# Meta keys inside the diagonal key blocks, and half-stored weights, in a planner-ordered trunk kernel

## The chip, the cores and the metric

The kernel runs on one core of one Trainium2 chip. TensorE multiplies matrices from SBUF into PSUM, VectorE, ScalarE and GpSimd do the elementwise work, and SyncE and GpSimd issue the DMAs. In the profile these are PE (with PEld for its weight loads), DVE, ACT, POOL and SP. The metric is the device time of one execution in microseconds (us); lower is better.

## The reference

One layer (DEPTH = 1) over 2048 tokens of width 1024, with 16 learned meta tokens put ahead of them. A combined projection gives seven groups of 512 columns. Half of the channels pass through GLU, a causal depthwise convolution, LayerNorm, swish, a second projection and a gate; the other half through stick-breaking attention with 8 heads of 64. Both halves are then projected, normalised and added to the input.

```python
def hybrid_layer(h, ...):
    u = rms_norm(h, pre_g)
    glu_a, glu_b, conv_gate, q, k, v, sb_gate = split(u @ w_in)
    c = glu_a * sigmoid(glu_b)
    c = causal_depthwise_conv(c, conv_w, conv_b)          # width 31
    c = silu(layer_norm(c, conv_ln_g, conv_ln_b))
    c = (c @ w_pw2 + b_pw2) * silu(conv_gate)
    s = stick_breaking_attention(q, k, v) * silu(sb_gate)
    return h + rms_norm(concat([c, s]) @ w_out, post_g)

# stick breaking, for every head, strictly causal (s < t):
#   z[t,s] = q[t].k[s] / 8
#   A[t,s] = sigmoid(z[t,s]) * prod_{s<j<t} (1 - sigmoid(z[t,j])) ;  out[t] = sum_s A[t,s] v[s]
```

The 16 meta tokens are the oldest keys of every query. The output drops their rows.

## The kernel before

**Tiles.** The 2048 tokens are four chunks `c` of 512 (`TC`), each of four token blocks `r` of 128. Every f32 operand of a matrix product is held as a rounded high part and the rest, the low part (fp32r), and a product takes three matmuls (high*high, low*high, high*low); `mm3` does this for the projections with a stationary weight of 128x128 and 512 moving columns. A weight slab of 128x512 is four such stationary operands.

**Attention.** `weigh` (L1291) takes one head, one key chunk `kc` and one query block `r`: two matmuls (q high, q low against `kk`, the stacked high and low keys) into a PSUM tile `T`, a sigmoid on ACT in place, and a scan on DVE from the newest key to the oldest that forms the running product `pr`. In the diagonal chunk (`kc == c`) only the first 128(r+1) keys count. `flip` turns the products by four PE transposes into another `T` tile, ACT copies the high part `ah` out, DVE subtracts for the low part `al`, and `gather` multiplies both by the differences of the values (`vk`) into `av`. PSUM has eight banks: two `mm`, four `T`, one `av`, one `cv`.

**Meta keys.** They are handled apart. `meta_k` (L1060) loads the meta keys once into `km`. When a pair of heads' queries has been projected, `meta_scores` (L935) multiplies them with `km`: two matmuls of 512 columns into a `T` tile, an ACT copy and a DVE addition into `zt`. In unit `i == 2` of each chunk's attention `zt` is turned by four transposes and copied by DVE to `sgm` (L1465). After all heads of a chunk have been weighed, `meta_keys` (L1500), which runs during the next chunk, takes the sigmoid of `sgm` on ACT, continues the scan over the 16 keys (four scans on DVE), turns the result into one `T` tile `pt`, and for each of four pairs `j` of heads reads 32 rows of `pt` twice: ACT copies the high part into a tile `mixs`, DVE subtracts for the low part; POOL copies the high part once more. Then one matmul against `vm` (the meta values) per pair. In the last chunk this is done in parts of heads (`ehl` instead of `mixs`), and for the last two heads in `meta_late`, which uses `vl`.

**Weights.** A raw slab comes by DMA into one of `RAWS` = 4 buffers `wr`; ACT rounds it to the high part, POOL (at the very start DVE) subtracts for the low part. Slabs used in several chunks are written back to DRAM (`wscr`, 512 KB: both parts) when first split in chunk 1's projections or chunk 0's tail, and later loaded from there straight into a `w` buffer, four of which exist. `prepare` (L560) does this for the next slab whenever one is released.

**Order.** The order of instructions is made while the program is built. Work on the PE comes as streams of pieces; `merge` (L1867) picks between attention (`main`), the projections (`fill`) and the meta keys (`extra`) by when, by a simple clock model with one cost per operation, the data and PSUM tiles of the next piece will be there. What follows on the other engines is put off by `when(...)` and let go in the order of that clock. Engines run their own queue in order, so the model's mistakes show as waits. Any change of a cost, a buffer or an operation moves many instructions after it. The stages of the program overlap: while chunk `c` is in attention, the fill is the gate of `c`, the output projection of `c-1`, the convolution's tail of `c` and the input projection of `c+1`. In chunk 3 the fill ends with `out_part`, the output projection as far as its inputs are there; `last_room` gives it the buffers of the projection's input.

All engine calls pass through one helper, so nearly every row of the profile has line 218; rows are told apart by tile names (`mm<-uh,w` is a projection, `T<-kk,q` the scores, `T<-ident,pr` the turning, `av<-ah,vk` the gathering).

Of the kernel before, what the change touches and what calls it, by code (L numbers as in the profile page):

```python
# [19 lines left out]
P = 128  # L20
# [19 lines left out]
EV, WB, RAWS, PR, EHL = 5, 4, 4, 9, 4  # L40
# [46 lines left out]
class Clock:  # L87
# [3 lines left out]
    def __init__(self):  # L91
        self.ready, self.used, self.free, self.rings, self.bufs = {}, {}, {}, {}, {}
        self.dma = 0.0
        self.shared = {}
        self.soon = []

        self.here = ()
# [71 lines left out]
class Engine:  # L169
# [7 lines left out]
    def __getattr__(self, name):  # L177
        call = getattr(self.engine, name)

        def issue(out, *args, **kw):  # L180
# [11 lines left out]
            when = max([c.at(a) for a in near] + [c.free.get(out.name, 0.0)]) + self.wait  # L192
            if self.gap:
# [12 lines left out]
            done = self.now + late  # L206
            if name == "dma_start":
# [15 lines left out]
def pe_cost(name, n, kw):  # L223
    return (0.108 if name == "transpose" else max(n * 4.537e-4, 0.11)), 0.19
# [42 lines left out]
def trunk(ctx: ExitStack, tc: tile.TileContext, x, xturn, xlater, meta, cpack, post_g, wpack, out):  # L267
# [84 lines left out]
    both = const.tile([P, ncp + TC], F32, name="cp")  # L352
    cp, zt = both[:, : ncp + KD * NM], both[:, ncp:]
# [31 lines left out]
    vl = const.tile([P, 2, P], F32R, name="vl")  # L385
    km = const.tile([P, NJ, 3, 2 * NM], F32R, name="km")
    cm = const.tile([P, NTB, NH, MS], F32, name="cm")
    sgm = const.tile([P, NTB, NH, MS], F32, name="sgm")
    ct = [const.tile([P, HIST + TC], F32, name=f"ct{j}") for j in range(NJ)]

    def clear():
        for j in range(NJ):
            nc.gpsimd.memset(ct[j][:, 0 : HIST - NM], 0.0)
        nc.gpsimd.memset(km.bitcast(F32), 0.0)
        nc.gpsimd.memset(vm.bitcast(F32), 0.0)
        nc.gpsimd.memset(vl.bitcast(F32), 0.0)
        nc.gpsimd.memset(cm, 0.0)
        nc.gpsimd.memset(sgm, 0.0)
# [134 lines left out]
    wscr = dr.tile([len(again), P, 2, 4 * P], F32, name="wscr")  # L533
    place = {key: wscr[i] for i, key in enumerate(again)}
# [13 lines left out]
    whole = [key for key, n, kept, save in order if not kept]  # L548
# [11 lines left out]
    def prepare(most=WB):  # L560

        while most and todo_w:
# [14 lines left out]
            if kept and tag == "w":  # L577
                sp.dma_start(both.bitcast(F32), place[key][:, :, :n])
            elif kept:
                for i, t in ((0, hi), (1, lo)):  # L580
                    sp.dma_start(t.bitcast(F32), place[key][:, i, :n])
            else:
# [4 lines left out]
                def keep_it(key=key, both=both, lo=lo):  # L587
                    when(lambda: pool.dma_start(place[key], both.bitcast(F32)), [lo])

                split(raws.popleft(), hi, lo, dve if first else pool, keep_it if save else None)  # L590
# [305 lines left out]
    def qk_proj(c, g, scr, with_meta):  # L896
        for j in range(NJ):
# [37 lines left out]
    def meta_scores(j, hi, lo):  # L935

        pt = PT("T", [P, TC])
        for i, t in ((0, hi), (1, lo)):
            pe.matmul(
                pt[: 4 * NM], km[:, j, i : i + 2].rearrange("p i s -> p (i s)"), t[:, NM:],  # L940
                start=(i == 0), stop=(i == 1),
            )
        zj = zt[2 * j * NM : 2 * (j + 1) * NM]
        act.activation(zj, pt[: 2 * NM], AF.Copy)
        dve.tensor_tensor(zj, pt[2 * NM : 4 * NM], zj, op=ALU.add)
# [54 lines left out]
    def values(c):  # L1000
# [3 lines left out]
        for j in range(NJ):  # L1004
# [52 lines left out]
            if c == 0 and j == 0:  # L1057
                in_us(4.5, meta_k, outs=[km])

    def meta_k():  # L1060
        force("k")
        for e in range(2):
            rows = slice(e * HD, (e + 1) * HD)
            for i in range(2):
                sp.dma_start(
                    km[rows, :, 1 - i, e * NM : (e + 1) * NM].bitcast(F32),
                    kscr[e::2, i, :, 0:NM].rearrange("j d s -> d j s"),
                )

    def meta_v(h):  # L1070
# [8 lines left out]
        if h >= EARLY:  # L1079
            sp.dma_start(  # L1080
                vl[h * NM : (h + 1) * NM, :, e * HD : (e + 1) * HD].bitcast(F32),
# [175 lines left out]
    def load_k(h, kc):  # L1257
        force("k")
        s0 = NM + kc * TC
        kk = T("kk", [P, TC], 2, F32R)  # L1260
        sp.dma_start(
            kk.bitcast(F32), kscr[h, :, :, s0 : s0 + TC].rearrange("l d s -> (l d) s")
        )
        return kk

    def load_first(c, force=False):

        if ("first", c) not in keep and (force or (("q", c) in keep and ("z", c - 1) in keep)):
            keep["first", c] = load_q(c, 0), load_k(0, c)
# [5 lines left out]
    def attention(c, mixs):  # L1275
        heads = {}

# [13 lines left out]
        def weigh(u, r):  # L1291
# [7 lines left out]
            z = PT("T", [P, TC])  # L1299
            for i in range(2):  # L1300
                pe.matmul(
                    z[:, :wd], hd["q2"][:, i, r * P : (r + 1) * P], kk[:, :wd],
                    start=(i == 0), stop=(i == 1),
                )
            act.activation(z[:, :wd], z[:, :wd], AF.Sigmoid, scale=-SCALE)
            pr = T("pr", [P, TC], PR)
            dve.tensor_tensor_scan(
                pr[:, :wd][:, ::-1], z[:, :wd][:, ::-1],
# [122 lines left out]
        for i in range(len(order) + 1):  # L1431
            u = None
            if i < len(order):
                h, kc = order[i]
                u = dict(h=h, kc=kc, diag=kc == c, kk=kk, a=[], at=[])
                if i + 1 < len(order):
                    if c == 0:
                        heads[h + 1] = load_q(c, h + 1)
                    kk = load_k(*order[i + 1])
                    if 0 < kc == c and h + 1 < NH:  # L1440
                        heads[h + 1] = load_q(c, h + 1)
            for b in range(NTB if u else len(flips)):
                if u:
                    yield need(heads[u["h"]]["q2"], u["kk"], tag="T")
# [593 lines left out]
```

## Time and profile before

| | |
|---|---|
| three runs | 1309.15, 1309.17, 1310.23 us; median 1309.17 |
| profiled execution | 1310.28 us, of it 1308.5 us span of the core |
| mean granted TensorE clock | 0.997 |
| DMA traffic | 300.83 MB, 230 GB/s on average |
| HBM written | 77.46 MB |

In the page, "busy" of an engine is the share of the span in which an instruction of it ran; matmuls are pipelined, so the PE's rows overlap and a matmul's own duration (some 0.39 us for 512 columns) is longer than the distance between two starts. That distance is read from the timeline. A row of the timeline gives the start, the length, the engine, line and operation, the tile written and the tiles read, the shape and the count of merged instructions; in brackets stands the idle time of the engine just before, and what ended it. A row of the groups gives the count, the busy time, the mean of one in ns, and after a second bar the idle time before these instructions with the releasers.

### The profile page before, as it was taken

Reading aid. Unit: us, or ns where it says so; the run is one execution under the profiler, and the core shown is the slowest. Engines: PE = TensorE matmul, PEld = TensorE weight load, DVE = VectorE, ACT = ScalarE, POOL = GpSimd, SP = SyncE. Lnnn points to the kernel's source line nnn. Section 1 sums busy time; section 2 is a strip of 40 time slices with the busy share of each in tenths; the row PEclk is TensorE's granted clock in tenths of the full one; section 3 lists DMA queues with packets and bytes.
Section 4 is the critical chain, followed back from the end, with each engine's and each line's share of the span. In section 5 each row is a group of like instructions: output and inputs, shape, how many; then the busy total and the mean of one; then the engine's idle time right before and its main releaser. Section 6 shows DMA issues by size and latency. Waiting matters only on the chain.

```text
span 1308.5 us, 21884 instructions
## 1 busy us (share of the span) xinstructions
PE 1284.4 (98%) x7442; PEld 1106.4 (85%) x7442; DVE 1019.2 (78%) x1446; ACT 743.0 (57%) x1477; POOL 690.4 (53%) x820
## 2 busy tenths in 40 slices
PE   8999999999899999999999999999999999999897
PEld 8998888888799878888789988888887899888797
DVE  5999999999873588974676578985558988898964
ACT  6544455444555452676645544688785666755543
POOL 3555568767687430878762232599887221321402
PEclk9999999999999999999999999999999999999999
DMA  6687877899868986667756696667666456586555
GB/s 234 216 277 236 264 252 258 300 348 314 287 218 285 322 289 199 202 214 231 252 166 194 193 344 208 184 197 215 213 200 213 138 157 199 180 259 212 177 164 183
DMA packets 166400, 300.83 MB, mean 230 GB/s; under 512 B 17280, under 2 KB 71744, under 8 KB 166288
## 3 DMA queue, kind: packets, MB, share of 16 engines
q1 hardware_dynamic: 152496, 251.44, 61.8%
q0 software_dynamic: 13792, 47.98, 9.5%
q8 instruction: 59, 0.97, 0.3%
q14 instruction: 53, 0.43, 0.1%
HBM read 221.90 MB, written 77.46 MB: 229 GB/s over the span
## 4 chain that ended last, share of the span: by engine, by line
PE 87%; DVE 5%; ACT 2%; DMA 2%; issue 2%; POOL 1%; SPq 1%; DVEq 0%; POOLq 0%; ACTq 0%
PE mm L218 57%; PE T L218 20%; PE av L218 9%; DVE pr L218 2%; DVE ul L218 1%; ACT ev L218 1%; DMA w<-wscr 1%; DVE sgm L218 1%; DMA wr<-wpack 1%; DVE tok L218 1%; SPq L218 1%; DVE mixs L218 0%; DMA qscr<-ehl 0%; POOL w L218 0%; PE cv L218 0%
## 5 line engine op out<-in xcount | busy, mean ns | idle before, releaser
L218 PE MATMUL mm<-uh,w 128*128 128x512 f32 (+1 forms) x1936 | 563.7, 377 | 1.1 <-ACT uh L218 1.1
L218 PEld LDWEIGHTS mm<-uh,w 128*128 128x128 f32 x1936 | 336.7, 188 | 53.5 <-ACT uh L218 1.7
L218 PE MATMUL mm<-ul,w 128*128 128x512 f32 (+1 forms) x968 | 357.6, 371 | 0.1
L218 DVE TENSOR_TENSOR al<-T,ah 128x512 fp32r<-128x512 f32 (+1 forms) x320 | 191.7, 599 | 119.2 <-ACT ah L218 117.8
L218 DVE TENSOR_TENSOR_SCAN pr<-T,pr,zcol 128x512 f32<-128x512 f32 x192 | 245.2, 1277 | 44.4 <-ACT T L218 42.8
L218 ACT ACTIVATE ah<-T 128x512 fp32r<-128x512 f32 (+1 forms) x320 | 170.1, 532 | 178.0 <-PE T L218 176.2
L218 DVE SCALAR_TENSOR_TENSOR cv<-ct,cp,cv 128x512 f32<-128x512 f32 x319 | 239.1, 749 | 7.0
L218 ACT ACTIVATE T<-T 128x512 f32<-128x512 f32 (+2 forms) x320 | 167.7, 525 | 84.3 <-PE T L218 73.9
L218 POOL TENSOR_TENSOR acc<-acc,pd 128x512 f32<-128x512 f32 x150 | 194.9, 1299 | 34.3 <-ACT pd L218 26.6
L218 POOL TENSOR_TENSOR w<-wr,w 128x512 fp32r<-128x512 f32 x132 | 171.2, 1303 | 75.2 <-ACT w L218 72.8
L218 PEld LDWEIGHTS mm<-ul,w 128*128 128x128 f32 x968 | 181.6, 188 | 33.6 <-DVE ul L218 0.5
L218 PE MATMUL T<-kk,q 128*128 128x512 f32 (+3 forms) x640 | 194.2, 386 | 3.7 <-DVE pr L218 2.6
L218 PE MATMUL T<-ident,pr 128*128 128x128 f32 x1088 | 171.9, 273 | 2.1 <-DVE al L218 1.1
L218 PEld LDWEIGHTS T<-ident,pr 128*128 128x128 f32 x1088 | 134.7, 141 | 33.7 <-DVE al L218 1.5
L218 PEld LDWEIGHTS T<-kk,q 128*128 128x128 f32 x640 | 105.9, 190 | 18.8 <-DVE pr L218 4.1
L218 DVE TENSOR_TENSOR_SCAN pr<-T,tri 128x128 f32<-128x128 f32 (+3 forms) x128 | 103.6, 814 | 22.9 <-ACT T L218 22.5
L218 ACT ACTIVATE pd<-ct,cp 128x512 f32<-128x512 f32 x150 | 106.7, 718 | 21.7 <-POOL acc L218 21.2
L218 PE MATMUL av<-ah,vk 128*128 128x512 f32 (+1 forms) x320 | 117.8, 368 | 0.0
L218 PE MATMUL av<-al,vk 128*128 128x512 f32 (+1 forms) x320 | 117.4, 367 | 0.0
L218 ACT ACTIVATE w<-wr 128x512 fp32r<-128x512 f32 x140 | 86.5, 626 | 33.7 <-POOL w L218 10.0
L218 POOL COPY cm<-pr 128x1 f32<-128x1 f32 x120 | 24.0, 200 | 131.7 <-DVE pr L218 131.1
L218 POOL TENSOR_TENSOR ev<-ev 64x512 f32<-64x512 f32 (+2 forms) x46 | 55.5, 1206 | 68.8 <-ACT ev L218 38.5
(210 smaller groups left out, 1609.7 us busy)
## 6 DMA issues: line engine op xcount, KB each, us to landing
w<-wscr SPq DMA_DIRECT2D x150, 512.0 KB, 4.1
wr<-wpack SPq DMA_DIRECT2D x140, 256.0 KB, 4.4
wscr<-w POOLq DMA_DIRECT2D x68, 512.0 KB, 5.0
kk<-kscr SPq DMA_DIRECT2D x80, 256.0 KB, 4.6
vk<-vscr SPq DMA_DIRECT2D x80, 256.0 KB, 3.9
q<-qscr SPq DMA_DIRECT2D x64, 256.0 KB, 5.8
vscr<-mixs SPq DMA_DIRECT2D x32, 256.0 KB, 3.4
qscr<-ehl SPq DMA_DIRECT2D x32, 256.0 KB, 3.4
```

The source lines that it names most:

```text
L218: return call(out, *args, **kw)
```

## The change

Five edits, which belong together in the building program:

1. **Meta keys as columns.** `km`, `zt`, `meta_k`, `meta_scores` and the turning of `zt` are gone. In the diagonal chunk `kk` gets 16 columns ahead of its 512, loaded from the same `kscr` (one DMA of 528 columns in chunk 0, where they are neighbours; a separate 16-column DMA in chunks 1 to 3). For `r` = 0, 1, 2 the score matmuls take 16 columns more in the same PSUM tile. For `r` = 3, where 512 columns fill the bank, each of the two parts has an extra matmul of 16 columns into a `T` tile of its own. ACT takes the sigmoid of the 16 columns straight into `sgm` (128x16), ahead of the large one; there are two `sgm`, one for even and one for odd chunks, and the later sigmoids over `sgm` are gone.
2. **Kept weights.** Of the input projection's kept slabs (all but the convolution gate's) only the low part is written (`lscr`, 256 KB) and read back; the raw slab is loaded again and ACT rounds it for the high part. The others keep both parts.
3. **Meta weights copied once.** For chunks 0 to 2 `meta_keys` copies `pt` to an SBUF tile (`turned`) by one ACT instruction of 128x512; high and low parts are formed from that.
4. **Five raw buffers** (`RAWS` = 5).
5. **Around them:** `vl` goes into unused rows of `vm`; in the last chunk the first part of `meta_keys` may begin when `last_room` has made room and waits for the convolution only before its matmuls, using two of that room's buffers; `out_part` takes the convolution's half of the first products for both token halves before the attention's half; the clock model lets an engine wait for another that holds the same PSUM bank, and prices a matmul by its own columns.

```diff
-EV, WB, RAWS, PR, EHL = 5, 4, 4, 9, 4
+EV, WB, RAWS, PR, EHL = 5, 4, 5, 9, 4
...
+            for b in banks:
+                who, end = c.last.get(b, (self, 0.0))
+                if who is not self:
+                    when = max(when, end)
...
+            if name == "matmul":
+                n = int(np.prod(out.shape[1:]))
...
-    return (0.108 if name == "transpose" else max(n * 4.537e-4, 0.11)), 0.19
+    return (0.108 if name == "transpose" else max(n * 4.537e-4, 0.11 if n > NM else 0.03)), 0.19
...
+    def low_alone(key):
+        return key[0] == w_in and key[1] // P // NJ * NJ != G_CG
...
-    whole = [key for key, n, kept, save in order if not kept]
+    whole = [key for key, n, kept, save in order if not kept or low_alone(key)]
...
+                raw = raws.popleft()
+                if kept:
+                    sp.dma_start(lo.bitcast(F32), place[key][:, :n])
+                    when(lambda raw=raw, hi=hi: act.activation(hi, raw, AF.Copy), [raw], [hi])
+                else:
+                    split(raw, hi, lo, dve if first else pool, keep_it if save else None)
...
-            if g == G_Q:
-                when(
-                    lambda a=(j, hi, lo): meta_scores(*a), [hi, lo], [zt], tag="T",
-                    date=pe.now + 4.0,
-                )
...
-            z = PT("T", [P, TC])
+            zb = PT("T", [P, TC])
+            o = NM if diag and wd < TC else 0
+            z, zr = zb[:, o : o + wd], zb[:, 0:NM]
+            if diag and not o:
+                zr = PT("T", [P, TC])[:, 0:NM]
             for i in range(2):
+                q = hd["q2"][:, i, r * P : (r + 1) * P]
+                if diag and not o:
+                    pe.matmul(zr, q, kk[:, 0:NM], start=(i == 0), stop=(i == 1))
                 pe.matmul(
-                    z[:, :wd], hd["q2"][:, i, r * P : (r + 1) * P], kk[:, :wd],
-                    start=(i == 0), stop=(i == 1),
+                    zb[:, : o + wd], q, kk[:, NM - o : NM + wd], start=(i == 0), stop=(i == 1)
                 )
-            act.activation(z[:, :wd], z[:, :wd], AF.Sigmoid, scale=-SCALE)
+            if diag:
+                act.activation(sgm[:, r, h, 0:NM], zr, AF.Sigmoid, scale=-SCALE)
+            act.activation(z, z, AF.Sigmoid, scale=-SCALE)
...
             if i == 2:
-                force(zt)
-                yield need(zt, tag="T")
-                pt = PT("T", [P, NTB, NH, NM])
-                for r in range(NTB):
-                    pe.transpose(
-                        pt[:, r].rearrange("p h s -> p (h s)"), zt[:, r * P : (r + 1) * P], ident
-                    )
-                dve.tensor_copy(sgm[:, :, :, 0:NM], pt)
...
+        turned = pt if part else T("ehl", [P, TC], EHL)
+        if not part:
+            act.activation(turned, pt, AF.Copy)
         for j in js:
-            src = pt[2 * j * NM : 2 * (j + 1) * NM]
+            src = turned[2 * j * NM : 2 * (j + 1) * NM]
...
-                for i in range(2):
-                    banks[i] = yield from out_products(
-                        w, mix, range(KD - 2), i, False, there=there
-                    )
+                for part in range(NJ), range(NJ, KD - 2):
+                    for i in range(2):
+                        banks[i] = yield from out_products(
+                            w, mix, part, i, False, banks[i], there
+                        )
```

Three places of the new order. First the PE where chunk 3's attention begins (one head's diagonal block, `q_...` being the queries), before:

```order
L218 MATMUL T<-kk,q_11175 128x256 x2
L218 MATMUL T<-kk,q_11175 128x384 x2
L218 MATMUL T<-kk,q_11175 128x512 x2
L218 MATMUL mm<-uh,w 128x512 x2
L218 MATMUL mm<-ul,w 128x512
L218 MATMUL mm<-uh,w 128x512 x2
L218 MATMUL mm<-ul,w 128x512
L218 MATMUL T<-ehl,km 64x512 x2
L218 MATMUL T<-kk,q_11175 128x512 x2
```

and the same place of the changed kernel:

```order
L228 MATMUL T<-kk,q_11477 128x272 x2
L228 MATMUL T<-kk,q_11477 128x400 x2
L228 MATMUL mm<-uh,w 128x512 x2
L228 MATMUL mm<-ul,w 128x512
L228 MATMUL mm<-uh,w 128x512 x2
L228 MATMUL mm<-ul,w 128x512
L228 MATMUL T<-kk,q_11477 128x16
L228 MATMUL T<-kk,q_11477 128x512
L228 MATMUL T<-kk,q_11477 128x16
L228 MATMUL T<-kk,q_11477 128x512 x5
```

The two matmuls against `km` have gone, the first three score pairs are 16 columns wider, and each half of the fourth has a 16-column matmul ahead of it.

Second, ACT where the meta weights of chunk 2 are taken out of PSUM (`mixs<-T 32x512` reads 32 rows of the turned tile; `ah` and `T<-T` are attention's own copies and sigmoids), before:

```order
L218 ACTIVATE ev<-mm 128x512
L218 ACTIVATE w<-wr 128x512
L218 ACTIVATE T<-T 128x512
L218 ACTIVATE mixs<-T 32x512 x4
L218 ACTIVATE ah<-T 128x512
L218 ACTIVATE T<-T 128x512
L218 ACTIVATE ah<-T 128x384
```

and now:

```order
L228 ACTIVATE w<-wr 128x512
L228 ACTIVATE pd<-ct_94,cp 128x512
L228 ACTIVATE ehl<-T 128x512
L228 ACTIVATE mixs<-ehl 32x512 x4
L228 ACTIVATE ah<-T 128x512
L228 ACTIVATE T<-T 128x512
L228 ACTIVATE ah<-T 128x384
```

One copy of the whole tile stands ahead, and the four pieces read SBUF instead of PSUM.

Third, the PE near the end, where head 7's diagonal block begins while the output projection fills in (`mm<-w,mixc` is the convolution's half of it, `mm<-wr,mixs` the attention's), before:

```order
L218 MATMUL mm<-w,mixc 128x256 x12
L218 MATMUL T<-ident,pr 128x128 x4
L218 MATMUL T<-kk,q_14065 128x128 x2
L218 MATMUL av<-ah,vk 128x512
L218 MATMUL av<-al,vk 128x512
L218 MATMUL T<-ident,pr 128x128 x4
L218 MATMUL T<-kk,q_14065 128x256 x2
L218 MATMUL av<-ah,vk 128x512
L218 MATMUL av<-al,vk 128x512
L218 MATMUL T<-ident,pr 128x128 x4
L218 MATMUL T<-ident,uh 128x128 x4
L218 MATMUL T<-kk,q_14065 128x384 x2
```

and now:

```order
L228 MATMUL mm<-w,mixc 128x256 x12
L228 MATMUL T<-ident,pr 128x128 x4
L228 MATMUL T<-kk,q_14432 128x144 x2
L228 MATMUL av<-ah,vk 128x512
L228 MATMUL av<-al,vk 128x512
L228 MATMUL T<-ident,pr 128x128 x4
L228 MATMUL mm<-w,mixc 128x256 x12
L228 MATMUL T<-ehl,vm 128x512
L228 MATMUL T<-ident,uh 128x128 x4
L228 MATMUL T<-kk,q_14432 128x272 x2
L228 MATMUL av<-ah,vk 128x512
L228 MATMUL av<-al,vk 128x512
```

Another group of twelve matmuls of the convolution's half now stands between the score blocks of this head.

More of the change, by code (lines that the diff above doesn't have):

```diff
@@ L94, in __init__ @@
         self.shared = {}
+        self.last = {}
         self.soon = []
@@ L192, in issue @@
             when = max([c.at(a) for a in near] + [c.free.get(out.name, 0.0)]) + self.wait
+            banks = [a.name for a in (*outs, *near) if a.space == PSUM]
+            for b in banks:
+                who, end = c.last.get(b, (self, 0.0))
+                if who is not self:
+                    when = max(when, end)
             if self.gap:
@@ L206, in issue @@
             done = self.now + late
+            for b in banks:
+                c.last[b] = self, self.now + 0.03
             if name == "dma_start":
@@ L351, in trunk @@
     ncp = NJ * CW + KD + 4 * NJ
-    both = const.tile([P, ncp + TC], F32, name="cp")
-    cp, zt = both[:, : ncp + KD * NM], both[:, ncp:]
+    cp = const.tile([P, ncp + KD * NM], F32, name="cp")
     cw = cp[:, 0 : NJ * CW].rearrange("p (j w) -> p j w", w=CW)
@@ L384, in trunk @@
     vm = const.tile([P, NJ, P], F32R, name="vm")
-    vl = const.tile([P, 2, P], F32R, name="vl")
-    km = const.tile([P, NJ, 3, 2 * NM], F32R, name="km")
     cm = const.tile([P, NTB, NH, MS], F32, name="cm")
-    sgm = const.tile([P, NTB, NH, MS], F32, name="sgm")
+    sgms = [const.tile([P, NTB, NH, MS], F32, name=f"sgm{i}") for i in range(2)]
     ct = [const.tile([P, HIST + TC], F32, name=f"ct{j}") for j in range(NJ)]
@@ L576, in prepare @@
                 hi, lo = (T(tag, [P, 4 * P], RAWS, F32R)[:, :n] for _ in range(2))
[L577 to L581, printed above, removed]
+            if kept and not low_alone(key):
+                if tag == "w":
+                    sp.dma_start(both.bitcast(F32), place[key][:, :, :n])
+                else:
+                    for i, t in ((0, hi), (1, lo)):
+                        sp.dma_start(t.bitcast(F32), place[key][:, i, :n])
             else:
@@ L1276, in attention @@
         heads = {}
+        sgm = sgms[c % 2]
         def load_v(h, kc):
@@ L1443, in attention @@
                 if u:
-                    yield need(heads[u["h"]]["q2"], u["kk"], tag="T")
+                    yield need(
+                        heads[u["h"]]["q2"], u["kk"], tag="T",
+                        n=2 if u["diag"] and b == NTB - 1 else 1,
+                    )
                     weigh(u, b)
@@ L1513, in meta_keys @@
             pool.memset(bm, 0.0)
+        sgm = sgms[c % 2]
         zm = sgm[:, :, hs, 0:NM]
-        act.activation(zm, zm, AF.Sigmoid, scale=-SCALE)
         for r in range(NTB):
@@ L1538, in fetch @@
         def fetch(j):
-            given[j] = [ev()[:, :TC] for _ in range(2)]
-            hold.update(t.name for t in given[j])
+            if j:
+                given[j] = [ev()[:, :TC] for _ in range(2)]
+                hold.update(t.name for t in given[j])
+            else:
+                given[j] = keep["first given"]
             bring(j)
@@ L1566, in meta_keys @@
             pool.tensor_copy(m[4 * NM : 6 * NM], m[high].bitcast(F32))
+        if part:
+            yield need(given=lambda: ("conv", c) in keep)
         for j in js:
@@ L1923, in last_room @@
         keep["bm"] = a[:, 4:6].rearrange("p e (b h s) -> p e b h s", b=NTB, h=NH)
+        keep["first given"] = a[:, 6], a[:, 7]
+        keep["room", c] = True
         pool.memset(a[:, 4:6], 0.0)
-        zm = sgm[:, :, EARLY:, 0:NM]
-        act.activation(zm, zm, AF.Sigmoid, scale=-SCALE)
         keep["pg"] = a[:, 2:4]
```

69 lines of the change are left out of this document (28 added, 41 removed).

## The prediction

> **What bounds the kernel now.** I read the page first: busy shares, slices, and the chain of work that ended last.
>
> ```profile
> PE 1284.4 (98%) x7442; PEld 1106.4 (85%) x7442; DVE 1019.2 (78%) x1446; ACT 743.0 (57%) x1477; POOL 690.4 (53%) x820
> ...
> PE   8999999999899999999999999999999999999897
> ...
> PE 87%; DVE 5%; ACT 2%; DMA 2%; issue 2%; POOL 1%; SPq 1%; DVEq 0%; POOLq 0%; ACTq 0%
> ```
>
> The PE is busy 98% of the span in every stage and holds 87% of the chain. So a microsecond is won in two ways only: by matmuls that go, or by moments in which the PE waits. What the other engines save counts where the PE waits for them. The waits of the PE, longest first in total, are short:
>
> ```profile
> PE T L218 <- DVE pr L218: 5.3, 6, 2.0
> PE T L218 <- DVE mixs L218: 4.2, 3, 2.5
> ```
>
> They are single events of up to 2.5 us, all for a tile `T`, so I looked each up in the timeline. The other terms are small too; a change here is worth about 1%.
>
> **Meta keys as columns: the PE's work.** The distance between starts, not a row's length, is what a matmul costs.
>
> ```profile
> 978.15 0.62 PE L218 MATMUL T<-ehl,km 128*64 128x512 f32 x2
> 978.61 0.62 PE L218 MATMUL T<-kk,q 128*128 128x512 f32 x2
> ...
> 1150.64 0.60 PE L218 MATMUL T<-ident,pr 128*128 128x128 f32 x4
> 1150.99 0.42 PE L218 MATMUL T<-kk,q 128*128 128x128 f32 x2
> 1151.25 0.44 PE L218 MATMUL av<-ah,vk 128*128 128x512 f32 x1
> ...
> L218 PE MATMUL T<-ehl,km 128*64 128x512 f32 x32 | 10.2, 399 | 2.5 <-DVE pr L218 2.5
> ```
>
> Two `km` matmuls take 978.61 - 978.15 = 0.46 us, so 0.23 us each, and 0.45 ns per column; 32 of them go: **-7.4 us**. Four transposes take 0.35 us; four groups of four go: **-1.4 us**. Added are 3 x 64 score matmuls wider by 16 columns: 192 x 16 x 0.45 ns = **+1.4 us**. Then 64 matmuls of 16 columns, one each of 32 heads and chunks for high and low. None is in the trace. By columns alone one costs 0.007 us; the nearest row is the pair of 128 columns, 0.26 us, or 0.13 each, of which 0.058 is columns and 0.07 is something a short matmul can't hide. I take 0.007 + 0.07 = 0.08: **+5.1 us**, with ends at 64 x 0.007 = 0.4 and 64 x 0.13 = 8.3. Together **-2.3 us** (-7.0 to +0.9). [...]
>
> The fourth block also needs a second `T` tile, 32 times; before, 16 score products and 4 turnings of `zt` needed one. A wash: the new tile is free after one short ACT row.
>
> **The waits at the old products.** Two of the longest waits stand at them:
>
> ```profile
> 338.15 2.37 DVE L218 TENSOR_TENSOR_SCAN sgm<-sgm,cm 128x136 f32<-128x136 f32 x4
> 338.30 0.63 PE L218 MATMUL T<-kk,q 128*128 128x512 f32 x2
> ...
> 340.88 0.68 PE L218 MATMUL T<-ehl,km 128*64 128x512 f32 x2 [1.96 <-DVE pr L218]
> 341.40 0.61 PE L218 MATMUL mm<-uh,w 128*128 128x512 f32 x2
> ...
> 638.60 0.68 PE L218 MATMUL T<-ehl,km 128*64 128x512 f32 x2 [0.56 <-DVE pr L218]
> ```
>
> Four meta scans (2.37 us) hold DVE, the attention scans stand behind them, no `T` is free, and the PE stops at `km`. That matmul goes and projections are next, which need no `T`: a gain of up to 1.96 + 0.56 = 2.5 us. The scans remain, though, so the next matmul that wants a `T` can be the one that is late. I take **-1.5 us** (-2.5 to 0).
>
> **Meta weights copied once.**
>
> ```profile
> L218 ACT ACTIVATE mixs<-T 32x512 fp32r<-32x512 f32 x12 | 7.1, 590 | 10.6 <-DVE mixs L218 9.3 <-PE T L218 1.2
> ...
> 988.00 0.59 ACT L218 ACTIVATE mixs<-T 32x512 fp32r<-32x512 f32 x1 [0.75 <-DVE mixs L218]
> 988.62 0.69 DVE L218 TENSOR_TENSOR mixs<-T,mixs 32x512 fp32r<-32x512 f32 x1 [0.66 <-ACT mixs L218]
> ...
> 989.34 0.59 ACT L218 ACTIVATE mixs<-T 32x512 fp32r<-32x512 f32 x1 [0.75 <-DVE mixs L218]
> ...
> 990.80 0.47 PE L218 MATMUL T<-mixs,vm 96*128 96x512 f32 x1 [2.46 <-DVE mixs L218]
> ...
> 349.77 0.47 PE L218 MATMUL T<-mixs,vm 96*128 96x512 f32 x1 [0.82 <-DVE mixs L218]
> 350.99 0.73 PE L218 MATMUL T<-kk,q 128*128 128x512 f32 x2 [0.75 <-DVE pr L218]
> 648.02 0.52 PE L218 MATMUL T<-ident,pr 128*128 128x128 f32 x3 [0.89 <-DVE mixs L218]
> ```
>
> ACT and DVE read the same PSUM tile in strict turn, each idle while the other reads: a pair takes 1.34 us (988.00 to 989.34), four take over 5 us, and all that attention wants of both engines stands behind. The PE pays at all three places: 0.82 + 0.75 + 0.89 + 2.46 = 4.9 us. After the change one ACT copy (some 0.6 us, as other 512-column copies) frees the `T` tile; ACT then does its four pieces of 0.59 without waiting, 0.6 + 4 x 0.59 = 3.0 us. The first weights are ready after about 0.6 + 0.6 + 0.7 = 1.9 us plus a queue, where the PE's order has 24 projection matmuls (5.5 us) between. I take **-4.5 us** (-4.9 to 0): the ACT block of 3.0 us in a row may still cost a little.
>
> **The end.** Head 7's attention waits with little beside it:
>
> ```profile
> 1224.78 0.48 PE L218 MATMUL T<-kk,q 128*128 128x256 f32 x2 [0.89 <-DVE ehl L218]
> ...
> 1226.81 0.66 PE L218 MATMUL T<-ident,pr 128*128 128x128 f32 x4 [1.09 <-DVE al L218]
> ...
> 1238.53 0.73 PE L218 MATMUL T<-kk,q 128*128 128x512 f32 x2 [1.01 <-DVE pr L218]
> ```
>
> These are 3.0 us. With the convolution's half of the first products taken first, for both token halves, more groups of twelve short matmuls can stand in such places, and the order shows them there. The parts' meta weights are still read in turn. I take **-2.0 us** (-3 to +1).
>
> **Kept weights, five raw blocks.** 40 writes shrink by 256 KB, 10.5 MB of 300.8; reads stay (256 raw + 256 low). No PE wait of weight hangs on a DMA, so I count nothing. The cost is on ACT: 80 more copies, and 128 short sigmoids:
>
> ```profile
> L218 ACT ACTIVATE w<-wr 128x512 fp32r<-128x512 f32 x140 | 86.5, 626 | 33.7 <-POOL w L218 10.0 <-PE mm L218 7.5 <-DMA wr<-wpack 7.0
> L218 ACT ACTIVATE row<-cv 128x16 f32<-128x16 f32 x1 | 0.2, 180 | 0.0
> L218 ACT ACTIVATE cp<-T 32x512 f32<-32x512 f32 x16 | 9.4, 588 | 19.1 <-PE T L218 19.0
> ```
>
> 80 x 0.626 + 128 x 0.18 = 50 + 23 us, less 9.4 and some 3 for the sigmoids: +61 us, ACT at 804 us, 62% of the span. The fullest stage is what counts, the projections of chunk 3:
>
> ```profile
> 880.00:900.00 20.00, 20.00 (x98) 16.36 (x97) 11.83 (x13) 16.88 (x29) 18.58 (x15) 1.00 0.76 231
> 900.00:920.00 20.00, 20.00 (x107) 16.75 (x106) 10.06 (x14) 16.39 (x31) 18.57 (x22) 1.00 0.70 220
> ...
> 1030.40 0.60 PE L218 MATMUL T<-ident,acc 128*128 128x128 f32 x4
> ```
>
> (The columns are PE, PEld, DVE, ACT, POOL, clock, DMA; the last row is the PE turning the first sums of chunk 3's convolution.) ACT has 16.9 of 20 us; some 40 copies over the 230 us from 750 on add 2 to 3 us per 20, so 95%. The cover is that the PE runs without a gap here at ACT's 84%, because projections need ACT only once in 5.6 us, and that ACT's convolution products can slide towards 1030, where the PE first wants their sum, and beyond it while the output projection fills in. I charge **+2.0 us** (0 to +13).
>
> **Sum:** -2.3 - 1.5 - 4.5 - 2.0 + 2.0 = -8.3 us on 1310.28 of the profiled execution (span 1308.5), 1302.0; its median of three runs is 1.1 lower, so **1300.9**, given as 1301.
>
> **Rivals.**
>
> *The waits move.* The order is made anew, and the freed moments are lost at other tiles; only the matmuls' -2.3 remain: 1306.9. For it: the meta scans still block DVE for 2.4 us in each chunk, and the model that sets the order puts them at less. Against: the longest waits hang on operations that are gone or halved. It lies at the edge between faster and unchanged.
>
> *ACT becomes the bound: slower.* A copy `w<-wr` that waits for its raw block holds everything behind it on ACT, sigmoids included, and so the PE's `T` tiles. The trace has the mechanism:
>
> ```profile
> 334.76 0.63 ACT L218 ACTIVATE w<-wr 128x512 fp32r<-128x512 f32 x1 [3.36 <-DMA wr<-wpack]
> ...
> ACT w L218 <- DMA wr<-wpack: 7.0, 4, 3.4
> ```
>
> Before, four of 140 copies waited so, 7.0 us in all, with ACT half idle. If in the full stages the 80 new copies (50 us) come through to the PE by more than a sixth (8.3 of 50), the gain is gone; at a quarter, 12.5 us more, the time is 1313.4. Against it: five raw blocks load ahead, and PE shows no wait there now. [...]
>
> *More than the sum.* Short matmuls hidden (-4.7 against my term), no charge on ACT (-2), all waits gone (about -2): 1301 - 8.7 = 1292.
>
> *The change does nothing:* the kernel stays within its waits, 1309. The `km` matmuls are gone from the order, so this needs 64 short matmuls at 0.13 us and new waits for all the old ones.
>
> **How the numbers follow.** Forecast 0.52 (1297 to 1305); waits move 0.20; slower by ACT 0.13; more than the sum 0.10; nothing 0.05. A measurement of this kernel tells about 0.2% (2.6 us) from no change, so 1306.6 to 1311.8 is "same". Of "waits move" half falls below 1306.6. Faster: 0.52 + 0.10 + 0.10 = 0.72; same: 0.10 + 0.05 = 0.15; slower 0.13. The range, 1294 to 1310, holds the forecast, moved waits, nothing, and the near part of the high gain.
>
> **What would show it.** Right: no long wait before `T<-mixs,vm`; ACT rows `mixs<-ehl` without idle time between; short `T<-kk,q` rows 0.05 to 0.1 us from their successor; PE waits of 1224 to 1238 shorter. Wrong: PE waits for ACT `w` or `T` between 500 and 1000 us with ACT over 95%; waits before `T<-kk,q` after the meta scans as long as now; a 16-column pair's block more than 0.26 us longer than an ordinary one.

## The result, and the profile after

The changed kernel takes **1302.42 us** (median of 4 runs, 1301.04 to 1302.80) where the kernel before takes 1309.16 (4 runs): a ratio of 0.9947, 95% interval 0.9930 to 0.9965. Six further runs (the experiment after_again) gave 1301.56 us, ratio 0.9935 (0.9923 to 0.9948). The forecast was 1301, in a range of 1294 to 1310. The profiled execution of after took 1302.12 us, 8.2 less than that of before.

First the page of after (busy time of each engine, and the granted clock in 40 slices), then the head of TensorE's list of waits (engine, tile, what it waited for: us in all, times, longest):

```profile
PE 1280.6 (98%) x7458; PEld 1108.8 (85%) x7458; DVE 1022.3 (79%) x1426; ACT 792.1 (61%) x1666; POOL 694.5 (53%) x819
...
PEclk9999998999999999999999999999999999999999
```

```profile
PE T L228 <- DVE al L228: 5.4, 4, 4.3
PE T L228 <- POOL ident masks.py:199: 1.8, 1, 1.8
```

The wait for `mixs`, 4.2 us before, is gone from the list. In its place stands one wait that before did not have, 4.3 us of TensorE for VectorE's `al`, and the slice in which it lies is the only one with a clock below 9 tenths. The total hides this: the change gained more than it shows, and gave about half of that back in one place.

To see where, I took every TensorE row and subtracted from the distance to the next row's start what the work itself takes by the usual distances of both traces: 0.4537 ns a column (232 ns for 512 columns), 109 ns for a transpose ahead of another, 28 ns for one ahead of something else. The sum of these is the work; what is left over (waits, half clock, what a short matmul takes beyond its columns) is counted by stretch, in us, rounded:

| | before | after | difference |
|---|---|---|---|
| work | 1231.3 | 1224.7 | -6.6 |
| left over, 0 to 150 us | 9.8 | 10.6 | +0.8 |
| 150 to 200 | 1.6 | 3.4 | +1.8 |
| **200 to 250** | 1.1 | 8.3 | **+7.2** |
| 250 to 750 | 22.7 | 18.9 | -3.8 |
| 750 to 950 | 6.0 | 7.6 | +1.6 |
| 950 to 1050 | 8.5 | 6.2 | -2.3 |
| 1050 to 1200 | 7.5 | 8.3 | +0.8 |
| **1200 to the end** | 11.1 | 3.9 | **-7.2** |
| ahead of the first row and behind the last | 9.0 | 8.4 | -0.6 |
| span | 1308.5 | 1300.3 | -8.2 |

In the column of after, what is left over also holds the 64 short matmuls, some 0.10 us each beyond their columns or 6.4 us in all (the price is measured below, under short_four_more): 3.4 us of it lie in the rows 250 to 750 and 950 to 1050, 1.0 in 750 to 950 and 0.8 in 150 to 250.

**The place between 200 and 250 us.** TensorE's rows around it in after (start, length, engine, line, operation, shape, count, and in brackets the idle time ahead and its releaser):

```profile
217.74 0.26 PE L228 MATMUL T<-kk,q 128*128 128x16 f32 x1
222.34 1.43 PE L228 MATMUL T<-kk,q 128*128 128x512 f32 x3 [4.34 <-DVE al L228]
223.57 0.31 PE L228 MATMUL av<-ah,vk 128*128 128x128 f32 x1
...
223.90 5.39 PE L228 MATMUL mm<-mixs,w 128*128 128x512 f32 x16
```

It is the new block of a diagonal (r = 3): the 16 meta columns are done, and the second `T` tile, for the 512 own keys, is not free, because VectorE has not yet subtracted `al` from it. Why VectorE is late, its own rows show, and GpSimd's beside them:

```profile
214.44 0.69 DVE L228 TENSOR_TENSOR_SCAN pr<-T,tri 128x256 f32<-128x256 f32 x1
215.04 5.19 DVE L228 COPY ct<-ct 128x30 f32<-128x30 f32 x1
220.34 0.69 DVE L228 TENSOR_TENSOR ct<-mm,ehl 128x512 f32<-128x512 f32 x1
...
221.60 0.68 DVE L228 TENSOR_TENSOR al<-T,ah 128x512 fp32r<-128x512 f32 x1
```

```profile
214.51 0.57 POOL L228 DMA_DIRECT2D wscr<-w  x1
215.11 1.30 POOL L228 TENSOR_TENSOR w<-wr,w 128x512 fp32r<-128x512 f32 x1
216.36 2.50 POOL L228 TENSOR_TENSOR mixs<-acc,mixs 128x512 fp32r<-128x512 f32 x2
218.80 0.18 POOL L228 COPY cm<-pr 128x1 f32<-128x1 f32 x1
218.94 1.25 POOL L228 TENSOR_TENSOR w<-wr,w 128x512 fp32r<-128x512 f32 x1
220.15 0.57 POOL L228 DMA_DIRECT2D wscr<-w  x1
```

The copy moves the last 30 columns of a convolution tile to its front (the history of the next chunk). Eight of the twelve in after take 0.16 to 0.18 us; this one takes 5.19, and it ends as GpSimd's unbroken row of SBUF instructions ends and a DMA issue comes. Then the price of the wait grows: the first seven of the 16 matmuls from 223.90 on start 0.43 us or more apart, where 0.23 is usual. Windows of after (length, then PE, PEld, DVE, ACT, POOL busy, clock, DMA share, GB/s) show the clock at 0.64 behind the wait; in each microsecond from 221 to 227 it is 0.50, the half clock meant here:

```profile
215.00:222.00 7.00, 3.00 (x20) 2.61 (x18) 6.90 (x5) 2.25 (x5) 5.70 (x7) 0.87 0.40 156
222.00:229.00 7.00, 6.66 (x21) 5.43 (x22) 5.56 (x8) 3.21 (x6) 3.16 (x6) 0.64 0.60 203
```

So one copy of 30 columns costs 4.3 us of waiting and, by (1 - 0.64) x 7, about 2.5 of half clock.

### The profile page after: what moved, and what is told of

Read it like the earlier page. It is cut to its first block, busy times and chain, and to the rows that moved or that the text cites. A ratio compares the mean times of both kernels' runs of the same rounds, so it can differ in the third digit from the quotient of the medians.

```text
span 1300.3 us, 22358 instructions
## 1 busy us (share of the span) xinstructions
PE 1280.6 (98%) x7458; PEld 1108.8 (85%) x7458; DVE 1022.3 (79%) x1426; ACT 792.1 (61%) x1666; POOL 694.5 (53%) x819
## 5 line engine op out<-in xcount | busy, mean ns | idle before, releaser
L228 PE MATMUL T<-kk,q 128*128 128x512 f32 (+4 forms) x704 | 201.2, 374 | 5.5 <-DVE al L228 4.9
L228 ACT ACTIVATE w<-wr 128x512 fp32r<-128x512 f32 x220 | 138.0, 628 | 95.9 <-PE mm L228 57.6
L228 PEld LDWEIGHTS T<-kk,q 128*128 128x128 f32 x704 | 115.2, 190 | 21.0 <-DVE al L228 5.8
L228 PE MATMUL mm<-w,mixc 128*128 128x256 f32 x600 | 81.2, 284 | 0.0
```

Of the source, the lines that this page charges most:

```text
L228: return call(out, *args, **kw)
```

## Experiments

All are compared with the kernel before on the same chip; 95% intervals of the ratio in brackets. The first run is the changed kernel once more, as the yardstick.

> The changed kernel itself, as the yardstick of the runs beside it: 1301 to 1303 us, 0.5% below the kernel before. If it comes out within 1 us of the four times shown, differences of 2 us between its variants can be read.

Measured: 1301.56 us (1299.61 to 1303.30), 0.9935 (0.9923 to 0.9948). Its trace has the same copy (5.20 us).

### The copy that stands still

The diffs of this part are written by what they do; in the kernels the engine is exchanged around the same line.

**hist_on_scalar:** the 12 history copies go to ScalarE; TensorE's order is the same row for row.

```diff
 # in pairs, the history ahead of the product
-dve.tensor_copy(ct[j][:, 0:HIST], ct[j][:, TC : TC + HIST])
+nc.scalar.activation(ct[j][:, 0:HIST], ct[j][:, TC : TC + HIST], AF.Copy)
```

(The planner still books VectorE's time for it, so that the order does not move; likewise in the next two.)

> The change with the 12 copies of the convolution's history (128 x 30 elements each) on ScalarE in place of VectorE; TensorE's order and GpSimd's stay the same row for row. Theory (the 4.34 us wait of TensorE at 222 us comes from such a copy, 5.19 us long where 0.17 is usual, which stands still on VectorE while GpSimd adds and subtracts from SBUF back to back): that wait is gone and the time is 4 to 5 us less, 1297 to 1299. Rival one (the stall is not the copy's: the next VectorE instruction with two operands in SBUF takes it over): VectorE stands still at the same place in another instruction, and the time is within 1 us of the changed kernel. Rival two (the stall was chance of that one execution): the changed kernel's median has it no more, and both are equal.

Measured: **1294.62 us** (1293.81 to 1295.33), 0.9885 (0.9872 to 0.9898): 6.9 us below the changed kernel beside it, more than the 4 to 5 expected. The wait is gone, and with it the half clock, which I had left out (the clock is 1.00 from 214 to 226 us). What was left over from 200 to 250 us fell from 8.9 in after_again to 1.6.

**hist_beside_psum:** the copies stay on VectorE at the same place, in a form with one operand from PSUM.

```diff
-dve.tensor_copy(hist, src)
+nc.vector.scalar_tensor_tensor(hist, pt[:, :HIST], 0.0, src, op0=ALU.mult, op1=ALU.add)
```

> The changed kernel with the 12 history copies still on VectorE and in the same places of every engine's order, but in another form: 0 times the projection in PSUM plus the history (scalar_tensor_tensor), so one operand comes from PSUM; the values are the same. Theory A (it is the form that stands still: a copy from SBUF to SBUF is held up by GpSimd's work on SBUF, an instruction that reads one operand from PSUM is not, as the convolution's cv<-ct,cp,cv rows with 0.75 us beside GpSimd's work show): no row of more than 0.5 us at 215 us, full clock at 222 us, and the time of the variant with the copies on ScalarE, 1294 to 1296. Theory B (any VectorE instruction at that place stands still): a row of 5 us there again and 1301 to 1303.

Measured: 1295.55 us (1295.08 to 1296.26), 0.9898 (0.9883 to 0.9913): theory A. The row at the same place, and the group of the twelve (busy us, mean ns after the bar):

```profile
215.09 0.17 DVE L311 SCALAR_TENSOR_TENSOR ct<-mm,ct 128x30 f32<-128x30 f32 x1
...
L311 DVE SCALAR_TENSOR_TENSOR ct<-mm,ct 128x30 f32<-128x30 f32 x12 | 2.2, 183 | 1.9 <-PE mm L228 1.7
```

Beside it the same group as a copy, in after, and after's convolution products, which also take one operand from PSUM (722 to 757 ns each):

```profile
L228 DVE SCALAR_TENSOR_TENSOR cv<-ct,cp,cv 128x512 f32<-128x512 f32 x319 | 239.1, 750 | 6.7
...
L228 DVE COPY ct<-ct 128x30 f32<-128x30 f32 x12 | 8.6, 717 | 0.0
```

The order, the place and the data are the same; only the form differs, and 717 ns become 183. It is the SBUF-to-SBUF copy that is held up, not the place in the queue.

**hist_before:** the edit of hist_on_scalar, made in the kernel before.

> The kernel before with its 12 history copies on ScalarE, TensorE's order the same. Theory A (the 5 us stall came with the change's new order, since the same copies last at most 1.09 us in the trace of before and nobody waits there): 0 to 1.5 us less than before, 1307.5 to 1310. Theory B (the copies cost as much before): 5 us or more less, below 1305.

Measured: 1308.28 us (1306.11 to 1310.87), 0.9993 (0.9983 to 1.0002), 1.0 us less than before: theory A. In the kernel before, the same copies lie at other places of GpSimd's work: the longest takes 1.09 us, and nobody waits for it. The stall came with the change's order.

**rule_undone:** the changed kernel without the PSUM bank rule of the model that sets the order.

```diff
 # Engine.issue
-                if who is not self:
-                    when = max(when, end)
```

> The changed kernel without the model's PSUM bank rule alone. Both kernels with the rule that were looked at for it (the change and the rule alone) have the 5 us copy at 215 us; the variant with the meta keys alone, without the rule, has none, but waits of 2.2 and 5.4 us at 315 and 349 us. Theory A (the rule is worth its order: the stall goes, other waits come): 1303 to 1312. Theory B (the rule only brings the stall): 1294 to 1297.

Measured: 1295.33 us (1292.11 to 1299.76), 0.9895 (0.9880 to 0.9911): theory B. The history copy there takes 0.77 us; GpSimd's row of SBUF work is cut by a DMA issue, and the copy's end (214.17) falls on it:

```profile
213.40 0.77 DVE L226 COPY ct<-ct 128x30 f32<-128x30 f32 x1
```

```profile
212.82 1.29 POOL L226 TENSOR_TENSOR w<-wr,w 128x512 fp32r<-128x512 f32 x1
214.05 0.57 POOL L226 DMA_DIRECT2D wscr<-w  x1
```

What was left over from 200 to 250 us is 1.8 in place of 8.3, and from 150 to 200 us 1.7 in place of 3.4. One new wait of 1.88 us, for a weight's DMA at 710 us, gives some of it back. So the change without one rule of its planner is 14 us faster than before, not 7.

### The parts alone and undone

**copy_alone** adds only the turned copy to the kernel before; **copy_undone** takes it out of the changed kernel.

```diff
 # meta_keys: copy_alone adds, copy_undone takes away
+        turned = pt if part else T("ehl", [P, TC], EHL)
+        if not part:
+            act.activation(turned, pt, AF.Copy)
-            src = pt[2 * j * NM : 2 * (j + 1) * NM]
+            src = turned[2 * j * NM : 2 * (j + 1) * NM]
```

> The kernel before with one edit of the change: ScalarE copies the turned meta weights out of PSUM once, and the heads' pieces are read from that copy. Theory A (the copy ends the waits before T<-mixs,vm, 4.9 us, and with them the stretch at 992 to 996 us in which the granted clock was 0.57 after these waits, 1.7 us): 4 to 6.5 us less than before, 1303 to 1305, and full clock from 990 to 1000 us. Theory B (what took the waits away in the changed kernel was its new order, since its variant without the copy is only 0.8 us slower): within 1.5 us of before, 1308 to 1310.

> The change without its turned copy: every head's piece of the meta weights is read out of PSUM by ScalarE and VectorE in turn again. Theory (the copy is worth the waits that it took away, 0.82 + 0.75 + 0.89 + 2.46 us before, 1.4 us of them left): 3 to 4 us more than the changed kernel, 1305 to 1306, with waits before the matmuls T<-mixs,vm back and ScalarE's mixs<- rows idle between. Rival (the order is made anew and those moments would be filled or lost elsewhere anyway): within 1 us of the changed kernel, 1301.5 to 1303.5, whether the waits come back or not.

Measured, copy_alone: 1307.29 us (1306.10 to 1311.68), 0.9988 (0.9977 to 0.9998), 2.4 us less than before; copy_undone: 1302.40 us (1300.25 to 1303.37), 0.9943 (0.9930 to 0.9956), 0.8 us above the changed kernel. For copy_undone the rival holds. For copy_alone neither theory does: the gain lies between them. In copy_alone the waits for the meta weights shrink as expected (what is left over falls by 2.6 us from 250 to 450 us and by 2.0 from 950 to 1050), and the clock is full at 992 us. But the remade order has three waits in chunk 1, 2.9 us, where before had one of 0.87 (left over from 450 to 600 us: 7.7 in place of 5.1):

```profile
485.09 0.73 PE L218 MATMUL T<-kk,q 128*128 128x512 f32 x2 [0.59 <-DVE pr L218]
...
487.54 0.55 PE L218 MATMUL T<-ident,pr 128*128 128x128 f32 x3 [1.26 <-DVE al L218]
...
491.82 0.44 PE L218 MATMUL T<-kk,q 128*128 128x128 f32 x2 [1.03 <-DVE pr L218]
```

```profile
483.00:493.00 10.00, 7.12 (x35) 5.04 (x34) 10.00 (x15) 7.37 (x14) 1.65 (x3) 1.00 0.31 100
```

(The window over them: VectorE busy throughout, TensorE 7.12 of 10 us, the clock full.)

In copy_undone no wait for the meta weights comes back: by the bank rule the planner knows that the pieces are read in turn, and puts projection matmuls there. In the changed kernel either of the two is enough.

**rule_alone:** only the bank rule, in the kernel before.

> The kernel before with one edit of the change: the model that sets the order lets an engine use a PSUM bank only after the other engine's access to it has ended, and nothing else. Theory A (the order that comes of it puts projection matmuls where TensorE waited for the meta weights; either this or the copy is enough): 4 to 6.5 us less than before, 1303 to 1305. Theory B (the rule alone only shuffles): within 2 us of before, 1307 to 1311, with the wait of 2.5 us before T<-mixs,vm still there.

Measured: **1320.54 us** (1317.50 to 1321.33), 1.0077 (1.0061 to 1.0092), 10.8 us slower: neither theory. Its order has the standing copy too, 5.52 us at the same moment, and at 363 us TensorE waits 3.26 us for VectorE's `mixs`, the meta weights: without the copy, the rule does not clear that place in this order. GpSimd's rows show that here the copy stood on past a DMA issue, through the next weight and up to the second issue:

```profile
215.03 5.52 DVE L226 COPY ct<-ct 128x30 f32<-128x30 f32 x1
```

```profile
218.64 0.56 POOL L226 DMA_DIRECT2D wscr<-w  x1
219.22 1.28 POOL L226 TENSOR_TENSOR w<-wr,w 128x512 fp32r<-128x512 f32 x1
220.44 0.56 POOL L226 DMA_DIRECT2D wscr<-w  x1
```

**keys_alone:** of the changed kernel only the meta columns are left (with the small moves in the tables that they need and the model's price of a matmul by its own columns); turned copy, kept low parts, fifth raw block, bank rule and the end's edits are undone.

> The changed kernel with only its first part left: meta keys as columns of the diagonal blocks. Undone are the turned copy, the kept low parts, the fifth raw block, the model's bank rule and both edits at the end. Theory of the prediction (matmuls -2.3, waits at the old meta scores -1.5, ScalarE's sigmoids nearly nothing): 3 to 4.5 us less than before, 1304.5 to 1306, if the 5 us copy of VectorE at 215 us does not occur in its order; with it and the slow clock behind it up to 7 us more, 1308 to 1312. Rival (the first part carries the whole gain): 1300.5 to 1303.

Measured: 1314.32 us (1313.31 to 1318.20), 1.0039 (1.0023 to 1.0054), 4.6 us slower than before and above everything that was expected. No standing copy (left over from 200 to 250 us: 1.7). The loss is 12.7 us more left over from 250 to 450 us, above all here:

```profile
354.39 2.05 PE L226 MATMUL T<-kk,q 128*128 128x512 f32 x4 [5.18 <-issue]
```

```profile
348.00:355.00 7.00, 1.82 (x11) 1.39 (x10) 2.81 (x5) 4.38 (x9) 3.02 (x6) 0.71 1.06 308
355.00:361.00 6.00, 5.63 (x16) 4.14 (x15) 6.00 (x8) 2.17 (x4) 5.67 (x9) 0.50 0.76 238
```

The profile names no releaser ("issue"), and the clock is at half behind the wait. The DMA engines are full in that window (1.06), but the two loads of the queries were issued at 343.3 and 344.1 and had landed by 352.6, 1.8 us before the wait ended. What ends with it is the reading of the meta weights: from 348.96 on ScalarE and VectorE read the turned tile in strict turn, four pieces each, and TensorE's row at 354.39 starts 0.10 us behind the end of the last one:

```profile
353.60 0.69 DVE L226 TENSOR_TENSOR mixs<-T,mixs 32x512 fp32r<-32x512 f32 x1 [0.66 <-ACT mixs L226]
```

So this is most likely the wait of before that the turned copy was meant to end, longer here; the times say so, a named releaser does not. The work itself is that of the changed kernel (1224.7 us).

**end_undone:** the two edits at the end are taken back.

```diff
 # meta_keys
-and (c < NCH - 1 or ("conv" if h0 else "room", c) in keep)
+and (c < NCH - 1 or ("conv", c) in keep)
 # out_part
-for part in range(NJ), range(NJ, KD - 2):
-    for i in range(2):
-        banks[i] = yield from out_products(w, mix, part, i, False, banks[i], there)
+for i in range(2):
+    banks[i] = yield from out_products(w, mix, range(KD - 2), i, False, there=there)
```

> The changed kernel with the two edits at the end undone: the output's first products in the old order (all six parts of one half, then of the other), and the early heads' meta weights only after the convolution's output. Theory (the end gained 7 us by them: 3.0 us of waits, and 1.8 us at a granted clock of 0.78 to 0.88 behind these waits): 4 to 7 us more than the changed kernel, 1306 to 1309, with waits of about 1 us between 1215 and 1240 us and the clock below 0.9 there. Rival (the end gained by the meta keys' own columns and the scores turned no more, and these edits are worth nothing): within 1.5 us of the changed kernel, 1300.5 to 1303.5.

Measured: 1307.14 us (1305.49 to 1310.55), 0.9977 (0.9966 to 0.9988): 5.6 us above the changed kernel, as the theory said. What is left over from 1200 us on goes from 3.9 to 9.9, nearly the 11.1 of before; nothing else moves by more than 0.5. The waits are short, but there are five of them in 9 us (three shown), and the clock falls behind them:

```profile
1224.57 0.47 PE L228 MATMUL T<-ehl,vm 96*128 96x512 f32 x1 [0.62 <-DVE al L228]
...
1228.23 0.66 PE L228 MATMUL T<-ident,pr 128*128 128x128 f32 x4 [0.66 <-DVE uh L228]
...
1230.27 1.03 PE L228 MATMUL av<-ehl,vm 128*128 128x512 f32 x2 [0.66 <-DVE ehl L228]
```

```profile
1221.00:1230.00 9.00, 6.36 (x33) 3.94 (x31) 8.95 (x13) 6.26 (x15) 5.62 (x5) 1.00 0.68 223
1230.00:1234.00 4.00, 3.73 (x13) 3.03 (x13) 3.37 (x9) 0.77 (x2) 2.01 (x4) 0.57 0.00 0
```

**kept_both:** both parts of kept weights are stored and loaded, as before; the five raw blocks stay.

```diff
 def low_alone(key):
-    return key[0] == w_in and key[1] // P // NJ * NJ != G_CG
+    return False
```

> The change with both parts of every kept weight stored and loaded again: 80 copies of 0.63 us (50 us) less on ScalarE, 10.5 MB more written. Theory of the prediction (+2.0 us for the copies on ScalarE): 2 us less, 1300 to 1301. Rival one (ScalarE's copies and the writes are both hidden, as the trace of the change shows between 800 and 950 us): within 1 us, 1301.5 to 1303.5. Rival two (fewer writes were a gain of their own, which the prediction counted as nothing): 2 us or more above the changed kernel, 1304.5 or more.

Measured: 1302.55 us (1301.66 to 1305.70), 0.9949 (0.9936 to 0.9962), 1.0 us above the changed kernel, its interval and that of the yardstick overlapping: rival one. 36 us less on ScalarE (755.6 busy in place of 792.1) and more bytes written give nothing that can be measured. The fifth raw buffer has no run of its own.

### The price of a short matmul

**short_four_more:** four more 16-column matmuls with the same weights ahead of each pair; the order of the rest stays.

```diff
 # weigh, r = 3 of a diagonal block
+                    if i == 0:
+                        for _ in range(4):
+                            pe.engine.matmul(zr, q, kk[:, 0:NM], start=True, stop=True)
```

> The changed kernel with four further 16-column matmuls ahead of each of the 32 pairs of them, 128 in all, back to back and with the same weights; the order of everything else stays. Theory A (such a matmul costs its start distance of 26 to 27 ns, and what the pair costs beyond that is the 512-column matmul behind it, which starts late): 128 x 0.027 = 3.5 us more than the changed kernel, 1305. Theory B (0.067 us each, the pair's cost halved): 8.6 us more, 1310. The prediction's 0.08: 10 us more, 1312.

Measured: 1315.70 us (1314.85 to 1316.47), 1.0050 (1.0037 to 1.0063): 14.1 us above the yardstick for 128 matmuls, 0.11 us each. All three expectations were too low. The starts tell why: where the short matmul follows a long one, the next starts 27 ns behind it, but from each further short one to the next it is 112 ns. The 27 ns are not the whole price in the changed kernel either, for the long matmul behind the short one then takes 313 ns to its successor, where 232 is usual. The fourth block behind a projection, without the pair (before) and with it (after):

```profile
978.61 0.62 PE L218 MATMUL T<-kk,q 128*128 128x512 f32 x2
979.08 0.62 PE L218 MATMUL mm<-uh,w 128*128 128x512 f32 x2
```

```profile
150.46 0.84 PE L228 MATMUL T<-kk,q 128*128 128x16 f32 x4
151.13 0.63 PE L228 MATMUL mm<-uh,w 128*128 128x512 f32 x2
```

(The row x4 is short, long, short, long.) With the pair the block takes 27 + 313 + 27 + 313 = 680 ns from start to start, without it 232 + 232 = 464, so 108 ns for each short matmul. Behind transposes, where the first matmul of a block takes longer in both kernels, it is 767 against 548, nearly the same. So a 16-column matmul costs about the same between long ones as in a row of its kind. The weight loads show the same distance: in after, the load for the first long matmul of the row above starts with the short one, at 150.46 us, and the load after it 109 ns later, at 150.57.

## Why the prediction was right, and where it was not

The time (1302.0 by the sum, 1302.12 in the profiled execution) came out by terms that were off in both directions. The places named were right; that the errors cancelled to a tenth of a microsecond was luck.

- **TensorE's work, -2.3.** Mis-sized, though inside its range. The work fell by 6.6 us, but the 64 short matmuls cost 64 x 0.108 = 6.9 us, of which 0.5 are in the work already: -0.2. The step that failed is the price of a short matmul: 0.08 was worked out from a pair of 128 columns, and 0.108 was measured. The pair's block is 0.216 us longer than an ordinary one, short of the 0.26 that was to show the price wrong.
- **Waits at the old meta scores, -1.5, and meta weights, -4.5.** Right in place, too small together, and wrong in how they came about. What is left over from 250 to 750 and from 950 to 1050 us fell by 3.8 + 2.3 = 6.1 us; 34 of the 64 short matmuls lie in these stretches, 3.4 us, so the waits and the half clock behind them lost about 9.5 where the two terms said 6.0. But the copy alone is not what earned it: undone, it costs 0.8 us; alone, it brings 2.4. The step that failed is the one that gave one edit the whole of the waits that it removes, with the order left as it was. The order is made anew from every duration: no order with the copy has a wait that VectorE's `mixs` ended, the rule without the copy clears these waits in copy_undone and not in rule_alone, and with neither (keys_alone) one of them most likely came to 5.18 us. No run takes the meta columns out of the changed kernel, so what they alone did for the old waits stays open. There was also a cost that the term left out: before, TensorE's wait of 2.46 us at 990 us was followed by half clock, as were the waits at the end:

```profile
988.00:992.00 4.00, 1.54 (x7) 1.05 (x6) 2.69 (x4) 3.19 (x6) 2.53 (x4) 1.00 0.32 117
992.00:996.00 4.00, 4.00 (x13) 3.08 (x12) 3.54 (x6) 2.49 (x5) 3.98 (x5) 0.57 0.39 123
1225.00:1230.00 5.00, 3.74 (x17) 2.77 (x17) 4.97 (x9) 3.32 (x8) 4.22 (x4) 0.78 0.52 165
1230.00:1235.00 5.00, 4.85 (x23) 3.66 (x21) 4.11 (x7) 2.66 (x6) 0.28 (x1) 0.88 0.13 37
```

- **The end, -2.0.** Right mechanism, mis-sized: -7.2 in the trace, and 5.6 us come back when the two edits are undone. The term counted three waits, 3.0 us. It left out the shorter waits around them and the half clock behind them, (1 - 0.78) x 5 + (1 - 0.88) x 5 = 1.7 us.
- **ScalarE's load, +2.0.** Too high: 0.6 at most in the stage that it was for. The copies and sigmoids came as counted (220 copies, 128 sigmoids), but in the fullest stage, 750 to 950 us, 1.0 of the 1.6 us more are the short matmuls of that stage, and in kept_both, with 80 copies fewer, it is 0.4 us less. TensorE still ran without a gap in the fullest windows, 840 to 920 us, and ScalarE did not come to the 95% of the charge: of the 20 us windows of after from 740 to 1000 the fullest, 940 to 960, has 17.60 us of its work.

```profile
L228 ACT ACTIVATE w<-wr 128x512 fp32r<-128x512 f32 x220 | 138.0, 628 | 95.9 <-PE mm L228 57.6 <-POOL w L228 12.0 <-issue 8.6
...
L228 ACT ACTIVATE sgm<-T 128x16 f32<-128x16 f32 x128 | 23.0, 180 | 32.3 <-PE T L228 31.9
```

- **What the sum lacked.** A cost of the new order itself: +7.2 us from 200 to 250 us, and +1.8 from 150 to 200 us (8.2 in all without the short matmuls), where two VectorE subtractions `ul` with both operands in SBUF stretch beside GpSimd in the same way (one lasts 3.49 us, the shortest of the eight 0.74). The rival "the waits move" had the kind right, but not the place, and the bank rule, which brings this order, had no term of its own. Without that rule the change would have come near the rival "more than the sum" (1295.3 measured, 1292 given).
- **The rivals.** ScalarE as the bound: against it stands kept_both. Nothing gained: against it stands the ratio.

In short: 8 us of stalls and half clock that the prediction did not see, and 2 us more for the short matmuls, were paid for by the waits (3.5 us more than counted), the end (5 more) and ScalarE's charge, of which at most 0.6 fell due.

## What to carry to other kernels

Where an order is computed from durations, an edit is worth what the whole new order is worth: here two parts of a change that gains 7 us cost 4.6 and 10.8 us alone, so a prediction needs a spread of some 10 us for the order, or the order's own stalls looked for one by one. Behind TensorE's waits of 2.46, 4.34 and 5.18 us, and behind five short ones within 9 us, the clock here was 0.57, 0.64, 0.50 and 0.57 in the windows of 4 to 7 us behind them; such waits have to be priced with that stretch. A matmul of few columns has to be priced at more than its columns: one of 16 columns took 0.11 us here, even between long ones. Small VectorE copies from SBUF to SBUF beside a busy GpSimd, one of which stood for 5.19 us here, can be worth moving to ScalarE or into a form that reads PSUM: **hist_on_scalar, at 1294.62 us, beats both kernels** by moving one copy to another engine, with TensorE's order left as it is.

## What the runs showed of the hardware

- An SBUF-to-SBUF copy of 30 columns on VectorE, 0.16 to 0.18 us at eight of its twelve places in after, stood for 5.2 to 5.5 us (after, rule_alone) while GpSimd worked on SBUF, through five or six of its instructions. It came free at a DMA issue of GpSimd in after and in rule_undone, but in rule_alone only at the second one; what lets it in stays open. In neither of the two long cases did it end between two of GpSimd's SBUF instructions.
- In after the granted clock fell within the wait of 4.34 us: it was 1.00 up to 220 us, 0.62 from 220 to 221 and 0.50 from 221 to 227, so it fell at about 220.2, 2.2 us behind the end of TensorE's last row (218.00). It also fell behind a wait of 2.46 us (before: 0.64 from 992 to 993 us, 0.50 from 993 to 995), and behind five waits of 0.4 to 0.7 us within 9 us (end_undone: TensorE busy for 6.36 of 9.00, then 0.57 from 1230 to 1234 us). In copy_alone, with TensorE busy for 7.12 us of the 10 from 483 to 493, it was 1.00 throughout those 10. So short waits that come together can count as well; where the limit lies, these runs do not show.
- A 16-column matmul costs 108 ns between long ones and 112 ns in a row of its kind.
